# Layer 0's output projection weights: split once beside the gates' projections and reloaded in two parts, instead of split inside the attention

## The chip, the cores and the metric

One core of one Trainium2 chip. The metric is the device time of one execution in microseconds; lower is better.

## The reference

A two-layer diffusion backbone over 2048 image tokens and 256 context tokens, 1024 wide, all in float32. Cut to what matters here, for layer 0:

```python
hx = rms_norm(x, norm_pre[0]) * (1.0 + sc_x) + sh_x      # the same for the context, hc
px = hx @ w_in                                           # 1024 -> 8 branches of 512
out_a = diff_attention_post(o, subln, lam_init) * silu(ga)   # o: differential attention, 8 heads,
                                                             # 2048 queries on 2304 keys
out_b = short_conv(bb, cb, ub, conv_w) * silu(gb)
mx = concat([out_a, out_b])                              # 1024 wide
x = x + g_x * rms_norm(mx @ w_out[0], norm_post[0])      # the output projection; the same for the context
```

The change concerns `w_out[0]`, a 1024 x 1024 float32 matrix (4.19 MB).

## The kernel before

**Two parts of a number.** Most large products run as three matmuls on float32r, a rounded float32: a matrix is split into a high part (rounded to float32r) and a low part (what is left), and the product is high x high + high x low + low x high. So each weight matrix has to be split before use: a rounding copy and a subtraction.

**Stages of layer 0.** `in_proj0` projects the inputs block by block; its last stage is the gates, 8 weight blocks of 128 columns times 5 chunks of tokens, 40 gate blocks in all, each 24 matmuls. `run` does them one after the other: `split_w` for a new weight block, `project`, then a step of the modulation and those steps of the context's small attention (`ctx_attention`) whose turn it is. PSUM has four buffers for the blocks; ScalarE (ACT) takes each out with a Silu, and a store on SyncE's (SP's) queue writes it to DRAM, for `ga` and `gb`.

`attention0` follows. Its order is written out by hand: `ATT_ORDER` gives each operation of a period of four query tiles a due time in ns, the period is `ATT_PERIOD` = 36858, and 32 periods cover 8 heads. The due times are only an order: they fix in which sequence each engine gets its instructions (`pin`). The operations are QK (score matmuls, L1044), TR (reduce_scores on VectorE, L803), EX (exponentials on ACT, L1083), PS and PA (GpSimd scales and adds, L1103 and L1108), TP and EV (transposes, L1115, and their copies on ACT, L1122), AV (values, L1132). Scores have two PSUM buffers, so a QK waits for the TR two before it. F are slots in which TensorE gets matmuls of the short convolution (`conv_units`, L734) until they are used up. Extra steps are put in by `run_late(d, step)`: due d ns after the present due time.

When the convolution is used up, `after_conv` is called (6000 after it). It frees the convolution's SBUF, calls `load_wout(0, ...)`, and puts in, by due time from the call: the 16 splits; the gate rows (`gate_rows`, two small matmuls that spread a row over the partitions); and the first context block of the output projection (`out_first`: nine calls, of which the first loads the mixed activations, `load_mix`, and casts them on VectorE at L1353 and L1355, and eight do three matmuls each at L1275). 37 TR operations are still to come after the call, the last due 54544 after it.

`load_wout` issues sixteen loads of 256 KB on SP's queue and returns sixteen splits. Each is one GpSimd copy (L1250) and one VectorE subtraction (L1251) of 128x512, pinned into these engines' orders among the attention's operations:

```python
self.pin(nc.gpsimd.tensor_scalar(h, x, 1.0, 1.0, ALU.mult, ALU.mult))
self.pin(nc.vector.tensor_tensor(lw, x, h.bitcast(F32), ALU.subtract))
```

After the last QK the rest of the context's output projection (`out_ctx`) and then that of the image tokens (`out_proj`) fill TensorE beside the attention's last transposes and values. `load_wout` is also used for layer 1, inside its own attention.

Each engine executes its instructions in order, and so does SP's queue, which issues every transfer of the kernel.

Of the kernel before, what the change touches and what calls it, by code (L numbers as in the profile page):

```python
# [9 lines left out]
F32 = mybir.dt.float32  # L10
F32R = mybir.dt.float32r
AF = mybir.ActivationFunctionType
ALU = mybir.AluOpType
# [4 lines left out]
P = 128  # L18
# [3 lines left out]
D = 1024  # L22
# [14 lines left out]


ATT_PERIOD = 36858
Y0 = 7000  # L40

FILL = 430

WGAP, YGAP = 1900, 3900
ATT_ORDER = """
QK0000:0 QK0001:349 TR0000:1266 TR0001:3756 QK0002:3791 TR0002:4792 QK0010:5725 LS000:5986 TR0010:6919 F00:6946
QK0011:7446 QK0012:8231 TR0011:8375 F01:8580 LX00:9023 EX000:9323 TR0012:9411 QK0100:9734 F02:10083 TR0100:10447
# [65 lines left out]
class _Tags:  # L113


    def __init__(self, pool, tags, bufs=None):
        self.pool, self.tags, self.bufs = pool, tags, bufs or {}
# [37 lines left out]
class Backbone:  # L155
    def __init__(self, ctx, tc, a):
        self.ctx, self.tc, self.nc, self.a = ctx, tc, tc.nc, a
        self.wout = None
        self.na = {}
        self.cst = ctx.enter_context(tc.tile_pool(reuse_waits="tile", name="cst", bufs=1))  # L160
        self.dram = ctx.enter_context(tc.tile_pool(reuse_waits="tile", name="dram", bufs=1, space=DRAM))
        d = self.dram

        self.q_hl = d.tile([2, BW, T], F32, name="q")
        self.k_hl = d.tile([2, BW, T], F32, name="k")
        self.v = d.tile([T, BW], F32, name="v")
        self.ga = d.tile([BW, T], F32, name="ga")

        self.mixa = [[d.tile([BW, n], F32, name=f"mixa{l}{t0}") for t0, n in CHUNKS[:5 - l]] for l in range(2)]
        self.mixb = [d.tile([BW, T - L * l], F32, name=f"mixb{l}") for l in range(2)]  # L170
        self.x1 = d.tile([S, D], F32, name="x1")
        self.hx0 = [d.tile([P, 2, 8, 256], F32, name=f"hx0{i}") for i in range(9)]
        self.hx1 = [d.tile([P, 8, 256], F32, name=f"hx1{i}") for i in range(9)]
        self.gb = d.tile([BW, T], F32, name="gb")
        self.q1_hl = [d.tile([BW, S], F32, name=f"q1{i}") for i in range(2)]
        self.k1_hl = [d.tile([BW, T], F32, name=f"k1{i}") for i in range(2)]
        self.v1 = d.tile([T, BW], F32, name="v1")
        self.gn = d.tile([BW, S], F32, name="gn")
        self.gd = d.tile([BW, S], F32, name="gd")
        self.fd = [d.tile([P, 4, 512], F32, name=f"fd{b}") for b in range(4)]  # L180
        self.bt = d.tile([8 * 64 * 15 * 64], F32, name="bt")
# [27 lines left out]
    def load(self, dst, src):  # L209

        self.pin(self.nc.sync.dma_start(dst, src))
# [236 lines left out]
    def split_values(self, src, ring, full, c, pin=None):  # L448
# [6 lines left out]
        nc.scalar.activation(wh, full, AF.Copy)  # L455
        nc.vector.tensor_tensor(wl, full, wh.bitcast(F32), ALU.subtract)


    def in_proj0(self, sil):
        MODS = 31  # L460
        nc, a = self.nc, self.a
        W = a["w_in_even"][0]
        with ExitStack() as es:
            tp = self.pool(es, "tmp0", 2, "left")
# [36 lines left out]
            def keep_hx(ci, part):  # L501

                t0, n, x = hx[ci][0], hx[ci][1], hx[ci][2 + part]
                for c0 in range(0, n, 256):
                    nc.sync.dma_start(self.hx0[(t0 + c0) // 256][:, part], x[:, :, c0:c0 + 256].bitcast(F32))
# [6 lines left out]
                return tp.tile([P, n, 256], F32, tag="wm", name=name)  # L512

            mod = self.modulation(mods, tp, mp, pt, wtile)
            ctx_steps = []
            loaded = []
            n_ctx = [0]
# [2 lines left out]
            def run(units):  # L520

                ws = {}
                for (b, w_ap, emit), ci in units:
                    if b not in ws:
                        ws[b] = self.split_w(w_ap, pw)
                        loaded.append(b)
                        nb = len(loaded)
                        with self.tc.issue_after(ws[b][2].ins):
                            if nb > 3 and keep:
                                keep_hx(*keep.pop(0))  # L530
                            if nb == 4:
                                self.bias_fill(tp)
                            if 8 <= nb < 16:
                                self.bias_rows(nb - 8)
                    self.project(ws[b], hx[ci], pp, emit, self.pin)

                    n_run[0] += 1
                    if n_run[0] > 45 or n_run[0] * MODS % 45 < MODS:
                        next(mod, None)
                    while ctx_steps and ctx_steps[0][0] < n_ctx[0]:  # L540
                        ctx_steps.pop(0)[1]()
                    n_ctx[0] += 1
# [68 lines left out]
            with self.tc.issue_after(self.pinned[mybir.EngineType.SP]):  # L611
                values(0, (2, 3))
                for ci in order[2:]:
                    make_hx(ci)
                    values(ci, range(4))
                block = lambda c0, emit: (c0, W[:, c0:c0 + P], emit)
                run([(block(1024 + 3 * P, store_v(3)), ci) for ci in order])
# [7 lines left out]
            def store_qk(dst, cb):  # L625
# [18 lines left out]
                return emit  # L644

            run([(block(512 + cb * P, store_qk(self.k_hl, cb)), ci) for cb in range(4) for ci in order])
            run([(block(cb * P, store_qk(self.q_hl, cb)), ci) for cb in range(4) for ci in order])
            rs.close()
            cp = self.pool(es, "ax", 1, "left")
            ctx_steps += self.ctx_attention(cp, pt)  # L650
            n_ctx[0] = 0

            def store_gate(dst, cb):
# [11 lines left out]

            run([(g, ci) for ci in (4, 1, 2, 0, 3) for g in gates[5:]])
            assert next(mod, None) is None
            assert not ctx_steps and not keep


# [279 lines left out]
    def attention0(self, ws, xs, ys, ps_t, ps_o):  # L950


        nc, a, tc = self.nc, self.a, self.tc
# [6 lines left out]
        with ExitStack() as es:  # L960
# [4 lines left out]
            sp = self.pool(es, "as", 1, "left")  # L965
# [14 lines left out]
            kst, qst, vts, nxt = {}, {}, {}, {}  # L980
# [22 lines left out]
            now, late, last, norms = [0], [], [], {}  # L1003

            def run_late(d, *steps):
                late.extend((now[0] + d, s) for s in steps)
                late.sort(key=lambda x: x[0])
# [179 lines left out]

            def after_conv():
                cs.close()
                fp, steps = self.load_wout(0, ws, xs)  # L1190
                rows = self.gate_rows(0, 1, _Tags(fp, {"grow": "ws"}, {"grow": 2}), ps_t, ep, "sq")
                first = self.out_first(_Tags(ep, {"m0": "ob", "m1": "ob"}, {"m0": 6, "m1": 6}))
                for i, step in enumerate(steps):
                    run_late(6000 + WGAP * i, step)
                for i in range(3):
                    run_late(6000 + 16 * WGAP + 1000 * i, lambda: next(rows, None))
                for i in range(9):
                    run_late(Y0 + YGAP * i, lambda: next(first, None))

# [23 lines left out]
                step()  # L1223
        return last


    def load_wout(self, l, es, fs):

        nc = self.nc
        wp = self.pool(es, f"ow{l}", 1, "right")  # L1230
        self.wout = ([], [])
        fp = self.pool(fs, f"of{l}", 1, "right")

        full = []
        for kc in range(8):
            for hf in range(2):
                x = (fp.tile([P, 512], F32, tag="ws", name="ws", bufs=2) if kc == 7 else
                     full[-1] if hf else wp.tile([P, D], F32, tag=f"wl{kc + 1}", name="ws"))
                cs = slice(hf * 512, hf * 512 + 512)
                full.append(x)  # L1240
                nc.sync.dma_start(x if kc == 7 else x[:, cs], self.a["w_out"][l][kc * P:kc * P + P, cs])

        def split(kc, hf):
            if hf == 0:
                self.wout[0].append(wp.tile([P, D], F32R, tag=f"wh{kc}", name="wh"))
                self.wout[1].append(wp.tile([P, D], F32R, tag=f"wl{kc}", name="wl"))
            cs = slice(hf * 512, hf * 512 + 512)
            h, lw = [self.wout[i][kc][:, cs] for i in range(2)]
            x = full[2 * kc + hf] if kc == 7 else full[2 * kc + hf][:, cs]
            self.pin(nc.gpsimd.tensor_scalar(h, x, 1.0, 1.0, ALU.mult, ALU.mult))  # L1250
            self.pin(nc.vector.tensor_tensor(lw, x, h.bitcast(F32), ALU.subtract))  # L1251

        return fp, [lambda kc=kc, hf=hf: split(kc, hf) for kc in range(8) for hf in range(2)]
# [804 lines left out]
```

## Time and profile before

| | us |
|---|---|
| median of 3 runs | 3311.87 (3310.3 to 3313.59) |
| the profiled execution | 3307.55 |
| its span, first to last instruction | 3305.8 |
| TensorE busy in the span | 3159.8 (96%) |
| VectorE busy | 1923.2 (58%) |
| ScalarE busy | 1588.4 (48%) |
| GpSimd busy | 1452.5 (44%) |

Layer 0's gates run from about 384 to 600 us of the span, its attention from 600 to about 1925; the convolution's last matmul starts at 1804.7, and load_wout's first load is issued at 1809.71. All rows come from the profiled execution, whose own time stands beside its span. A busy share over the whole span is a mean over stages with different limits.

### The profile page before, as it was taken

Reading aid. Unit: us, or ns where it says so; the run is one execution under the profiler, and the core shown is the slowest. Engines: PE = TensorE matmul, PEld = TensorE weight load, DVE = VectorE, ACT = ScalarE, POOL = GpSimd, SP = SyncE. Lnnn points to the kernel's source line nnn. Section 1 sums busy time; section 2 is a strip of 40 time slices with the busy share of each in tenths; the row PEclk is TensorE's granted clock in tenths of the full one; section 3 lists DMA queues with packets and bytes.
Section 4 is the critical chain, followed back from the end, with each engine's and each line's share of the span. In section 5 each row is a group of like instructions: output and inputs, shape, how many; then the busy total and the mean of one; then the engine's idle time right before and its main releaser. Section 6 shows DMA issues by size and latency. Waiting matters only on the chain. (4 is left out here: it accounts for less than half of the span.)

```text
span 3305.8 us, 53754 instructions
## 1 busy us (share of the span) xinstructions
PE 3159.8 (96%) x20154; PEld 2614.0 (79%) x20154; DVE 1923.2 (58%) x4315; ACT 1588.4 (48%) x2541; POOL 1452.5 (44%) x1205
## 2 busy tenths in 40 slices
PE   7999999999999999989999799999999998899999
PEld 6988878778787878777777578898888887788887
DVE  4466663688888888888887745321121026566643
ACT  4311143577777878777777543421111124566410
POOL 3234200477887888777877743200121002343300
PEclk9999999999999999999999899999999999999999
DMA  7367643523333243323332144533232247953233
GB/s 259 125 209 238 213 147 117 177 100 112 132 118 118 90 157 98 123 91 114 117 98 76 52 157 157 178 106 126 70 112 95 90 147 223 226 146 107 69 136 121
DMA packets 305319, 442.08 MB, mean 134 GB/s; under 512 B 54838, under 2 KB 212002, under 8 KB 292259
## 3 DMA queue, kind: packets, MB, share of 16 engines
q1 hardware_dynamic: 305058, 438.64, 41.2%
q8 instruction: 160, 2.62, 0.3%
q14 instruction: 101, 0.82, 0.1%
HBM read 307.59 MB, written 131.43 MB: 133 GB/s over the span
## 5 line engine op out<-in xcount | busy, mean ns | idle before, releaser
L421 PE MATMUL mm<-hx,wh 128*128 128x512 f32 (+1 forms) x2784 | 828.9, 381 | 2.3 <-DVE lo L631 2.3
L803 DVE CUSTOM_DVE_ANT_0 s<-ps,zero 128x768 f32<-128x768 f32 x768 | 718.2, 952 | 167.2 <-PE ps L1044 161.9
L1108 POOL TENSOR_TENSOR s<-s 128x992 f32<-128x992 f32 x256 | 595.4, 2340 | 7.2
L421 PEld LDWEIGHTS mm<-hx,wh 128*128 128x128 f32 x2784 | 509.3, 188 | 108.9 <-DVE lo L631 2.7
L421 PE MATMUL mm<-hx,wl 128*128 128x512 f32 (+1 forms) x1392 | 529.6, 380 | 0.0
L1044 PE MATMUL ps<-kst,qst 128*128 128x512 f32 (+1 forms) x1536 | 430.4, 369 | 75.4 <-DVE mx L803 67.4
L1122 ACT ACTIVATE aT<-pt 128x512 f32<-128x512 f32 (+1 forms) x640 | 336.2, 549 | 151.7 <-PE pt L1115 150.5
L1103 POOL TENSOR_SCALAR s<-s,cf 128x992 f32<-128x992 f32 x256 | 300.7, 1185 | 244.3 <-DVE cf L1093 114.5
L734 PE MATMUL cmm<-cx,wh 128*128 128x256 f32 x1728 | 355.2, 292 | 6.1 <-ACT z L753 4.9
L1044 PEld LDWEIGHTS ps<-kst,qst 128*128 128x128 f32 x1536 | 237.3, 193 | 143.0 <-DVE mx L803 90.4
L1115 PE MATMUL pt<-sm,s 128*128 128x128 f32 x2304 | 340.0, 277 | 5.9 <-ACT aT L1122 5.4
L1083 ACT ACTIVATE s<-s,bias 128x2304 f32<-128x2304 f32 x128 | 284.4, 2221 | 52.6 <-DVE bias L1072 52.3
L421 PEld LDWEIGHTS mm<-hx,wl 128*128 128x128 f32 x1392 | 262.1, 188 | 53.7
L1115 PEld LDWEIGHTS pt<-sm,s 128*128 128x128 f32 x2304 | 270.5, 142 | 42.1 <-ACT aT L1122 13.0
L734 PEld LDWEIGHTS cmm<-cx,wh 128*128 128x128 f32 x1728 | 278.1, 193 | 17.5 <-ACT z L753 7.9
L1083 ACT ACTIVATE s<-s,low 128x2304 f32<-128x2304 f32 x128 | 283.5, 2215 | 2.1
L1132 PE MATMUL po<-aT,vt 128*64 128x256 f32 x2304 | 278.3, 386 | 0.8 <-DVE f L827 0.8
L734 PE MATMUL cmm<-cx,wl 128*128 128x256 f32 x864 | 249.1, 288 | 0.0
L1132 PEld LDWEIGHTS po<-aT,vt 128*64 128x64 f32 x2304 | 154.3, 137 | 94.5 <-issue 27.2
L1934 POOL TENSOR_SCALAR s<-s,rz 128x832 f32<-128x832 f32 (+1 forms) x128 | 123.0, 961 | 200.2 <-DVE rz L1933 148.7
L1275 PE MATMUL y<-wh,mh 128*128 128x512 f32 x544 | 182.5, 414 | 1.2 <-DVE mx L803 1.2
L1275 PE MATMUL y<-wh,mx 128*128 128x512 f32 x544 | 173.9, 398 | 0.0
(265 smaller groups left out, 4802.0 us busy)
## 6 DMA issues: line engine op xcount, KB each, us to landing
cx<-hx SPq DMA_DIRECT2D x72, 1024.0 KB
hx<-hx SPq DMA_DIRECT2D x18, 1024.0 KB
kst<-k SPq DMA_DIRECT2D x192, 96.0 KB
k<-k SPq DMA_DIRECT2D x32, 576.0 KB
xt<-in_x_dram SPq DMA_DIRECT2D x32, 512.0 KB
wm<-in_w_mod_dram SPq DMA_DIRECT2D x64, 256.0 KB
qst<-q SPq DMA_DIRECT2D x256, 64.0 KB
ws<-in_w_in_even_dram SPq DMA_DIRECT2D x27, 512.0 KB
```

The costliest lines, as they stand in the source:

```text
L421: mm = self.nc.tensor.matmul(ps[:, :n], p[:, kc], y, start=first, stop=last)
L734: yield nc.tensor.matmul(ps, w[p][:, kc, :], x[q][:, kc, :], start=i == 0, stop=i == 23)
L803: return self.nc.vector.tensor_tensor_reduce(dst, ps, self.zero.to_broadcast([P, n]), -QS, BIGGEST, ALU.add, ALU.min, mx)
L1044: pin(nc.tensor.matmul(ps[:, k0:k1], q[:, qc:qc + P], k[:, k0:k1], start=True, stop=True))
L1083: pin(nc.scalar.activation(it.s[m], it.s[m], AF.Exp, bias=bias, scale=-1.0, accum_out=it.Z if m else it.rz[:, 0:1]))
L1103: pin(nc.gpsimd.tensor_scalar(x, x, it.cf, 1.0, ALU.mult, ALU.mult))
L1108: pin(nc.gpsimd.tensor_tensor(it.s[0][:, cs], it.s[0][:, cs], it.s[1][:, cs], ALU.add))
L1115: pin(nc.tensor.transpose(pt[:, i * P:i * P + P], it.s[0][:, k0:k0 + P], self.ident))
L1122: pin(nc.scalar.activation(it.aT[g][:, 0:k, n * P:n * P + P], it.pt.pop(g)[:, 0:k * P].rearrange("p (k q) -> p k q", q=P), AF.Copy))
L1132: pin(nc.tensor.matmul(it.po[c:c + 64, 0:256], vts[it.h][:, kt, :], it.aT[g][:, i, :], start=kt < 2, stop=kt >= 16, tile_position=(0, c)))
L1275: self.pin(self.nc.tensor.matmul(ps[hf] if isinstance(ps, list) else ps[:, cs], x, w[kc][:, cs], start=kc == 0 and i == 0, stop=kc == 7 an ...
L1934: nc.gpsimd.tensor_scalar(s[:, :w], s[:, :w], rz, 1.0, ALU.mult, ALU.mult).ins]
```

## The change

- `in_proj0` gets a new generator, `split_later`, called once after each gate block. It walks over `w_out[0]` in 32 chunks of 128x256: the load of the next chunk is issued a step ahead into one of two halves of a staging tile; ACT rounds the present chunk into a high part (one buffer); VectorE subtracts in place for the low part; two stores write the parts to DRAM.
- `after_conv` calls `load_wout0` instead of `load_wout(0, ...)`: sixteen loads of 512 KB, high and low part of each of the eight row blocks, straight to their places. The sixteen splits inside the attention are gone. Layer 1 keeps `load_wout`.
- The due times of the first context block's steps change: `Y0` from 7000 to 8000, `YGAP` from 3900 to 4500. The gate rows are now due at a fixed place of the attention's period, which comes to 31628, 32628 and 33628 after the call instead of 36400, 37400 and 38400.

```diff
-Y0 = 7000
+Y0 = 8000
-WGAP, YGAP = 1900, 3900
+WGAP, YGAP = 2000, 4500
@@ Backbone.__init__
+        self.wo_hl = [[d.tile([P, D], F32, name=f"wo{kc}{p}") for p in range(2)] for kc in range(8)]
@@
+    def split_later(self, sp, tp):
+        nc = self.nc
+        todo = [(self.a["w_out"][0][kc * P:kc * P + P, c0:c0 + 256], [x[:, c0:c0 + 256] for x in self.wo_hl[kc]])
+                for kc in range(8) for c0 in range(0, D, 256)]
+        def load(i):
+            x = place[:, i % 2 * 256:i % 2 * 256 + 256]
+            nc.sync.dma_start(x, todo[i][0])
+            return x
+        place = tp.tile([P, 512], F32, tag="eh", name="sl", bufs=1)
+        nxt = load(0)
+        yield
+        for i, (_, dst) in enumerate(todo):
+            full, hi = nxt, sp.tile([P, 256], F32R, tag="sl1", name="sl", bufs=1)
+            if i + 1 < len(todo):
+                nxt = load(i + 1)
+            lo = full.bitcast(F32R)
+            nc.scalar.activation(hi, full, AF.Copy)
+            nc.vector.tensor_tensor(lo, full, hi.bitcast(F32), ALU.subtract)
+            for x, y in zip(dst, (hi, lo)):
+                nc.sync.dma_start(x, y.bitcast(F32))
+            yield
@@ in_proj0
+            parts = iter(())
                     self.project(ws[b], hx[ci], pp, emit, self.pin)
+                    next(parts, None)
             ctx_steps += self.ctx_attention(cp, pt)
+            parts = self.split_later(self.pool(es, "sl", 1, "left"), tp)
             assert next(mod, None) is None
+            for _ in parts:
+                pass
@@ after_conv
-                fp, steps = self.load_wout(0, ws, xs)
+                fp = self.load_wout0(ws, xs)
-                for i, step in enumerate(steps):
-                    run_late(6000 + WGAP * i, step)
+                d = WGAP + (13000 - now[0] - WGAP) % ATT_PERIOD
                 for i in range(3):
-                    run_late(6000 + 16 * WGAP + 1000 * i, lambda: next(rows, None))
+                    run_late(d + 1000 * i, lambda: next(rows, None))
@@
+    def load_wout0(self, es, fs):
+        wp = self.pool(es, "ow0", 1, "right")
+        self.wout = ([], [])
+        for kc in range(8):
+            for i, t in enumerate(("wh", "wl")):
+                x = wp.tile([P, D], F32R, tag=f"{t}{kc}", name=t)
+                self.nc.sync.dma_start(x.bitcast(F32), self.wo_hl[kc][i])
+                self.wout[i].append(x)
+        return self.pool(fs, "of0", 1, "right")
```

## Rows read from the trace of the kernel before

**Rows 1.** The page, part 1: busy us (share of the span) and instructions.

```profile
PE 3159.8 (96%) x20154; PEld 2614.0 (79%) x20154; DVE 1923.2 (58%) x4315; ACT 1588.4 (48%) x2541; POOL 1452.5 (44%) x1205
```

**Rows 2.** Busy us by stretch: PE, PEld, DVE, ACT, POOL; granted clock, DMA share, GB/s.

```profile
1804.70:1816.10 11.40, 10.31 (x71) 7.56 (x69) 10.11 (x26) 10.79 (x15) 10.68 (x8) 1.00 0.51 173
1811.00:1891.20 80.20, 57.83 (x329) 40.27 (x327) 65.63 (x130) 48.08 (x72) 61.33 (x44) 0.89 0.20 66
1877.70:1891.20 13.50, 10.63 (x72) 7.47 (x70) 11.91 (x32) 11.12 (x19) 10.45 (x7) 1.00 0.02 5
1891.20:1932.00 40.80, 39.98 (x233) 29.39 (x234) 15.66 (x27) 17.14 (x32) 23.07 (x19) 1.00 0.36 125
```

**Rows 3.** Waits from 1804 to 1891: us in total, times, longest.

```profile
PE ps L1044 <- DVE mx L803: 19.1, 17, 4.2
...
DVE wl L1251 <- POOL wh L1250: 5.7, 5, 1.4
```

**Rows 4.** Groups by line, VectorE, 1811 to 1891.2: busy us, mean ns, idle before.

```profile
L803 DVE CUSTOM_DVE_ANT_0 s<-ps,zero 128x768 f32<-128x768 f32 x37 | 34.5, 951 | 5.8 <-PE ps L1044 5.7
L1251 DVE TENSOR_TENSOR wl<-ws,wh 128x512 fp32r<-128x512 f32 x16 | 21.7, 1355 | 5.7 <-POOL wh L1250 5.7
```

**Rows 5.** Groups by line, GpSimd, 1811 to 1891.2.

```profile
L1108 POOL TENSOR_TENSOR s<-s 128x992 f32<-128x992 f32 x13 | 29.8, 2303 | 0.2
...
L1250 POOL TENSOR_SCALAR wh<-ws 128x512 fp32r<-128x512 f32 x16 | 13.3, 837 | 0.0
```

**Rows 6.** VectorE in order of time: start us, us.

```profile
1819.44 0.69 DVE L1251 TENSOR_TENSOR wl<-ws,wh 128x512 fp32r<-128x512 f32 x1
...
1827.33 1.17 DVE L1353 CAST mh<-mx 128x512 fp32r<-128x512 f32 x1
...
1853.17 2.76 DVE L1251 TENSOR_TENSOR wl<-ws,wh 128x512 fp32r<-128x512 f32 x1 [1.24 <-POOL wh L1250]
```

**Rows 7.** GpSimd in order of time.

```profile
1853.10 2.27 POOL L1108 TENSOR_TENSOR s<-s 128x992 f32<-128x992 f32 x1
```

**Rows 8.** 5 us stretches, the same columns.

```profile
1810.00:1815.00 5.00, 4.79 (x37) 3.30 (x36) 3.75 (x10) 4.56 (x8) 4.92 (x4) 1.00 0.87 299
1815.00:1820.00 5.00, 4.47 (x33) 2.66 (x31) 3.60 (x10) 3.23 (x6) 3.97 (x4) 1.00 0.92 305
1820.00:1825.00 5.00, 2.63 (x13) 1.73 (x13) 4.18 (x6) 3.20 (x5) 5.00 (x5) 1.00 1.06 374
...
1830.00:1835.00 5.00, 3.97 (x17) 3.43 (x18) 3.92 (x9) 1.33 (x3) 2.29 (x3) 0.59 0.02 3
...
1850.00:1855.00 5.00, 2.27 (x15) 1.60 (x13) 3.73 (x6) 3.85 (x6) 5.00 (x4) 0.95 0.01 2
```

**Rows 9.** SyncE's queue in order of time.

```profile
1809.71 10.47 SPq L1241 DMA_DIRECT2D ws<-in_w_out_dram  x16
1820.53 0.38 SPq L1351 DMA_DIRECT2D mx<-mixb  x1
```

**Rows 10.** Groups by line, whole span: 128x256 copy and subtraction.

```profile
L695 ACT ACTIVATE wh<-ws 128x256 fp32r<-128x256 f32 (+1 forms) x37 | 13.3, 425 | 2.3 <-PE cmm L734 1.5 <-DMA ws<-in_w_in_even_dram 0.8
...
L631 DVE TENSOR_TENSOR lo<-mm,hi 128x256 fp32r<-128x256 f32 x8 | 3.4, 423 | 22.7 <-ACT hi L630 9.9 <-DMA k<-t 7.2 <-DMA q<-t 5.6
```

**Rows 11.** Stretches of layer 0's gates.

```profile
400.00:420.00 20.00, 15.88 (x73) 12.64 (x73) 12.05 (x39) 7.96 (x16) 0.00 (x0) 0.94 0.81 247
...
440.00:460.00 20.00, 20.00 (x97) 16.18 (x96) 12.31 (x41) 7.83 (x16) 0.00 (x0) 1.00 0.45 138
...
580.00:600.00 20.00, 20.00 (x89) 16.16 (x88) 1.65 (x2) 3.54 (x5) 0.74 (x1) 1.00 0.82 234
```

**Rows 12.** ScalarE in order of time, and what ended its idle time.

```profile
406.79 0.60 ACT L656 ACTIVATE g<-mm 128x512 f32<-128x512 f32 x1 [6.14 <-DMA ga<-g]
```

**Rows 13.** TensorE in order of time.

```profile
414.33 0.41 PE L916 MATMUL cpt<-sm,cs 128*128 128x128 f32 x2 [1.43 <-DVE czi L904]
417.42 0.62 PE L916 MATMUL cpt<-sm,cs 128*128 128x128 f32 x2 [2.68 <-DVE cs L907]
```

## The prediction

> **What bounds the kernel now.** I read the page first. TensorE (PE) is busy 96% of the span [rows 1], so work taken from another engine pays only where PE waits for that engine. I therefore looked along the span for the stretch where PE is not full and the edited lines run. The table by stretches gives it [rows 2]: from 1811.0 to 1891.2 us PE is busy 57.83 of 80.2 us, and the granted clock averages 0.89. Right after, from 1891.2 to 1932.0, PE is busy 39.98 of 40.8. So the 80.2 us are a trough between two full stretches, and what shortens the trough brings everything behind it forward. This is the end of layer 0's attention: the short convolution that filled PE is used up at 1804.7, and the output projection has not begun except for its first row block.
>
> Inside the trough PE waits for VectorE (DVE): score matmuls (L1044) wait for DVE's reduction L803, which frees their PSUM bank, 19.1 us in 17 waits, and DVE itself waits 5.7 us for GpSimd (POOL) at L1251 [rows 3]. By line DVE has 37 reductions, 34.5 us, and 16 weight subtractions L1251, 21.7 us [rows 4]; POOL spends 13.3 us on the 16 rounding copies L1250 besides its attention work [rows 5]. These 32 instructions are load_wout's split, and they are pinned into the two engines' orders among the attention's.
>
> The subtraction has two prices: 0.69 us alone, and 2.76 us at 1853.17 [rows 6], which is 0.69 plus almost the whole 2.27 us addition that POOL started at 1853.10 [rows 7]. DMA was at a share of 0.01 then [rows 8], so DMA traffic did not stretch it.
>
> **The change part by part.**
>
> *The split leaves the trough.* DVE loses 21.7 us of work and 5.7 us of waits there, 27.4 us; POOL loses 13.3. What is left over the 80.2 us, from the stretch's row [rows 2]: DVE 65.63-21.7 = 43.9, POOL 61.33-13.3 = 48.0, ACT 48.1, and PE 57.83 x 0.89 = 51.5 at the full clock. The clock fell to 0.59 in 1830-1835 [rows 8], a mix of the two levels of 1.2 and 2.4 GHz, while PE had waits in the trough, and those waits go. PE is then the longest, and the trough cannot be shorter than 51.5 us: the gain is at most 28.7. How full will PE be? From 1804.7 to 1816.1, with the convolution gone and the split not yet on DVE, it was busy 10.31 of 11.4 us, 90%; at the end, 1877.7 to 1891.2, with no split but the pipeline just refilling, 10.63 of 13.5, 79% [rows 2]. At 90% the trough is 57 us and the gain 23; at 79% it is 65.4 and the gain 14.8. I take 90%, because the first stretch is the same steady mix without the disputed work, and the second follows a stall. Term: -23, bounds -28.7 and -14.8.
>
> *Twice the bytes.* The sixteen 256 KB loads become sixteen of 512 KB, 8.39 MB where 4.19 were. Before, issuing starts at 1809.71 [rows 9], and DMA moves 299, 305 and 374 GB/s in the three 5 us stretches, mean 326 [rows 8]. At that rate the last weights land about 25.7 us after 1809.7, near 1835.4. PE needs them later: the first row block's eight steps are due 12.5 to 44 us after the loads' call (Y0 + YGAP i; all of the attention's remaining reductions fall within 54.5 us of it), about 1824 to 1857 at a 57 us trough, and its first pair of 1.05 MB lands after 3.2 us. So weights cost PE nothing; if that cover of 11 us at the first step were gone, the step would hold PE for what is missing.
>
> What is late next is the convolution's half of that row block: its load is issued behind the weights in the same queue (at 1820.53, after the sixteen) [rows 9], and so lands near 1836 where it was usable at 1827.33, when DVE's cast took it without waiting [rows 6]. DVE works in order: if the cast stands in its queue ahead of that landing, the reductions behind it wait, and the score matmuls behind those. The order after the change is not in this trace. Bounds: 0 if the cast stands behind the landing; about 13 if it keeps the place it had, eight reductions after the loads' start, which a faster trough reaches near 1823. In this kernel the cast came about 2 us after the traffic ended [rows 6, 8], so I place it near the landing: +2.
>
> The Trainium skill (DMA: Bandwidth & Descriptors, Specifications) gives 358 GB/s as HBM's limit for one core. By it 8.65 MB would take 24.2 us, an estimate, and land near 1834; the traced mean lands it near 1836, so the two differ by 2 us in this one term. A second page (SBUF — State Buffer, Who interferes with whom) says that engines and DMA cannot contend in SBUF, while DVE and POOL can lock each other out of a shared port pair. The trace agrees, 2.76 us at a DMA share of 0.01; were it otherwise, some 11 us of doubled traffic would also slow the reductions.
>
> *Retiming.* The first block's steps spread over 44 instead of 38.2 us, and the gate rows (two outer products and their casts) move from 36.4 to about 31.6 us behind the call. It is the same work inside the trough, already in the 51.5: 0.
>
> *The split beside the gates.* 32 steps, one after each of the first gate blocks: a 128 KB load one step ahead, an ACT copy of 128x256 (0.43 us by the convolution's weights), a DVE subtraction (0.42 by the same shape and operation) [rows 10], two 128 KB stores. That is 13.6 us of ACT and 13.4 of DVE spread over some 180 us in which PE is full: 20.00 of 20 in 440-460, with DVE 12.31, ACT 7.83 and DMA share 0.45, and so on to 580-600 [rows 11]. PE has four PSUM banks of slack, so the arithmetic is hidden. The queue is less free. SP issues 96 more transfers, in order with the gates' stores, the modulation's loads and the context attention's small loads, and 12.6 MB are added. At 400-420 DMA is already at 0.81 and PE busy only 15.88 of 20 [rows 11]: ACT stood 6.14 us until a gate store had landed [rows 12], and the context attention's transposes then held PE 1.43 and 2.68 us, 4.1 together [rows 13]. In the split a chunk's high part has one buffer, so each ACT copy waits for the previous store. With a round trip like that one, 6.14 + 0.43 = 6.6 us per step against about 5.4 for a gate block (24 matmuls; 89 run in the 20 us of 580-600 [rows 11]), ACT loses some 1.2 us a step while the queue is crowded. For the 3.7 steps of that 20 us stretch it is 4.4 us of ACT, and at the row's ratio (4.1 of PE for 6.14 of ACT) 3 us of PE. Afterwards, at 0.45, I expect none. Bounds 0 and, if every step loses 1.2 us, 32 x 1.2 x 4.1/6.14 = 26. I take +3.
>
> *Sum.* -23 + 2 + 3 = -18. The profiled execution took 3307.55 us against a span of 3305.8; the median of the runs shown is 3311.87, 4.3 above it. I subtract from both: 3289.6 for an execution like the profiled one, 3294 for the median.
>
> **The rivals.**
> 1. *The doubled loads hold DVE.* The cast stands early and DVE waits up to 13 us in the trough, so the gain is 23 - 13 - 3 = 7, some 3305. For it: one queue, in order, twice the bytes. Against: the cast did not wait before.
> 2. *SP's queue in the gate stage.* The one that ends slower. Each split step holds ACT behind its own store, and the context attention passes it to PE at 4.1 us for each 6.14 of ACT. From six such holds on (24.6 us) it outweighs the gain of 23; if all 32 steps lose 1.2 us and the trough gains only 14.8, the result is 26 + 2 - 14.8 = +13, near 3325. For it: the 400-420 stretch. Against: PE is full in each of the eight 20 us stretches from 440 to 600, and the first and the last leave ACT more than half idle [rows 11].
> 3. *The trough does not shorten.* POOL and ACT (48 us each) are in lockstep with PE, and removing the split turns DVE's work into waits for them; the gain is under 5 and the kernel lands near 3308 to 3312. For it: the chain of an attention tile passes all four engines. Against: the 90% stretch.
>
> **How the numbers follow.** Likeliest (trough down 15 to 28, small costs) 0.66; rival 1 0.14, of which 0.11 is still past the 0.2% that a measurement of this kernel can tell from no change (6.6 us); rival 2 0.12, 0.07 slower and 0.05 within 0.2%; rival 3 0.08, 0.03 of it faster. Faster is 0.66 + 0.11 + 0.03 = 0.80, same 0.03 + 0.05 + 0.05 = 0.13, slower 0.07. The low end takes the floor of PE with little cost, -27: 3285; the high end takes rivals 1 and half of 3, 3309. The likeliest case alone is 3285 to 3302.
>
> **What would show it.** Right: no L1250 or L1251 work in layer 0's trough, the last reduction L803 55 to 62 us after the loads start instead of 81, PE's waits on L803 there under 10 us, granted clock above 0.95, and everything behind shifted by the same amount. The weights' traffic lasts some 26 us. In the gate stage, PE's idle time grows by 0 to 6 us over the 4.1. Wrong: DVE idle before the cast until DMA lands (rival 1); ACT or SP waiting on the split's own stores, and attention starting 10 us or more later (rival 2); PE as idle as before but waiting for ACT's copies L1122 or POOL's sums L1108 (rival 3).

## The result and the profile after

The changed kernel took 3329.43 us (median of 6 runs, 3325.76 to 3334.42) against 3312.73 for the kernel before on the same chip (6 runs, 3304.98 to 3317.66): a ratio of 1.0054 [1.0041, 1.0068], slower by 0.54%. The forecast was 3294, the range 3285 to 3309: wrong in sign. The profiled execution took 3325.76 us, its span 3324.0, which is 18.2 above the 3305.8 of before.

Read in the stretches in which the prediction argued, the 18.2 us fall apart like this (us, before to after):

| stretch | before | after | difference |
|---|---|---|---|
| span's start to the first gate Silu | 384.0 | 390.6 | +6.6 |
| first to last gate Silu (the gate stage) | 219.8 | 260.9 | +41.1 |
| to the first QK | 0.6 | 0.7 | +0.1 |
| first QK to the convolution's last matmul | 1200.2 | 1192.7 | -7.5 |
| from there to the last reduction (the trough) | 85.6 | 65.0 | -20.6 |
| to the end | 1415.6 | 1414.1 | -1.5 |

**The trough.** The kernel after, stretches (us; busy us of PE, PEld, DVE, ACT, POOL; granted clock, DMA share, GB/s): first the end of the convolution, then from 1.3 us after the weights' first load, then the time of the loads and 5 us out of its middle:

```profile
1845.10:1856.60 11.50, 10.30 (x71) 7.56 (x70) 10.06 (x26) 10.88 (x15) 10.78 (x8) 1.00 0.58 203
1851.30:1910.90 59.60, 51.80 (x328) 37.18 (x326) 48.60 (x113) 47.67 (x72) 47.73 (x28) 0.97 0.42 159
1850.00:1874.50 24.50, 23.05 (x161) 16.52 (x161) 18.75 (x48) 21.32 (x32) 22.37 (x13) 1.00 0.98 375
1860.00:1865.00 5.00, 4.07 (x25) 3.02 (x24) 4.46 (x11) 4.75 (x10) 4.79 (x3) 1.00 1.02 415
```

Its waits from 1851.3 to 1910.9 (us in total, times, longest):

```profile
PE ps L1077 <- DVE mx L836: 5.2, 6, 2.5
```

The same operations in order of time, on SyncE's queue and on VectorE (two views):

```profile
1850.01 0.32 SPq L1267 DMA_DIRECT2D wh<-wo  x1
...
1863.43 0.32 SPq L1267 DMA_DIRECT2D wl<-wo  x1
1864.71 0.37 SPq L1395 DMA_DIRECT2D mx<-mixb  x1
```

```profile
1877.38 0.76 DVE L1397 CAST mh<-mx 128x512 fp32r<-128x512 f32 x1
```

Against [rows 2] DVE's load fell from 65.63 us in 80.2 to 48.60 in 59.6, PE is busy 87% instead of 72%, the clock is 0.97 instead of 0.89, and PE's wait for the reductions fell from 19.1 us [rows 3] to 5.2. While the doubled loads (8.39 MB) ran, all traffic of the core came to 375 GB/s over 24.5 us, and the cast behind them took its input without a wait.

**The gate stage.** Stretches of the whole stage, the kernel before and then the kernel after:

```profile
384.00:603.80 219.80, 215.55 (x1090) 176.28 (x1089) 100.17 (x317) 78.53 (x156) 8.30 (x10) 0.99 0.52 159
```

```profile
390.60:651.50 260.90, 228.47 (x1091) 184.85 (x1089) 113.11 (x349) 89.67 (x187) 7.41 (x10) 0.93 0.60 182
```

PE's idle time grew from 4.3 to 32.4 us, by 28.2. The other 12.9 of the 41.1 are in PE's busy time: the same matmuls took longer at a lower granted clock. By 20 us, the kernel after, answering to [rows 11]:

```profile
400.00:420.00 20.00, 12.78 (x65) 10.92 (x64) 9.88 (x31) 3.82 (x9) 0.00 (x0) 0.76 0.72 214
...
480.00:500.00 20.00, 13.88 (x73) 11.05 (x72) 11.44 (x35) 9.83 (x21) 1.12 (x1) 0.83 0.70 207
...
560.00:580.00 20.00, 13.21 (x64) 11.69 (x64) 9.72 (x32) 6.04 (x15) 1.01 (x1) 0.73 0.52 162
```

Of the stage's rows these three are the ones in which PE stood longest, and none has a lower clock (a mix of 1.2 and 2.4 GHz). What it stood for, from the waits of 380 to 660, first all engines, then SyncE's queue:

```profile
ACT sl L480 <- DMA wo<-sl: 63.9, 19, 8.8
DVE sl L481 <- ACT sl L480: 55.7, 21, 4.8
...
ACT wh L406 <- DMA ws<-in_w_in_even_dram: 17.2, 4, 6.5
...
PE cps L927 <- DMA cqk<-k: 12.0, 3, 7.2
...
PE cpt L949 <- DVE cs L940: 10.1, 5, 5.8
...
PE mm L423 <- ACT wh L406: 4.0, 3, 3.1
```

```profile
SPq L690 <- ACT g L687: 14.5, 9, 5.2
SPq L468 <- DMA wo<-sl: 13.7, 15, 3.2
SPq L483 <- ACT sl L480: 13.3, 9, 3.3
```

The waits of rival 2 are there: ACT stands 63.9 us behind the split's own stores. But the largest of PE's own waits, 12.0 us, is for something else, the context attention's small loads `cqk`. Next come 10.1 us of the context attention's transposes waiting for DVE, the kind of hold that the prediction priced (4.1 before [rows 13]), and 4.0 us in which the gates' own matmuls wait for the split of their weights, whose loads `ws` stand in SyncE's queue too. `cqk` by tile, the kernel before and then the kernel after (count; duration in ns min/median/max; first and last start; "who waited for it"):

```profile
L798 SPq DMA_DIRECT2D cqk<-k x64: 302/420/977, 385.6 to 524.7; - x64
...
who waited for it (us, times):
  DVE cs L803: 7.2, 2
```

```profile
L831 SPq DMA_DIRECT2D cqk<-k x64: 302/420/1539, 393.2 to 562.7; - x64
...
who waited for it (us, times):
  PE cps L927: 13.5, 4
  PEld cps L927: 9.2, 2
```

No matmul waited for them before; now PE and its weight loads do, 13.5 and 9.2 us, and the last one is issued 38.0 us later. (The two waits can overlap: in run 8 they add to 27.1 us where PE idles 24.3. So their sum is no share of PE's idle time.) Why it is late stands in SyncE's queue in order of time; below it TensorE at the same place:

```profile
407.50 0.46 SPq L287 DMA_DIRECT2D wm<-in_w_mod_dram  x1
408.00 0.97 SPq L831 DMA_DIRECT2D cqk<-q  x2
409.80 0.35 SPq L468 DMA_DIRECT2D sl<-in_w_out_dram  x1
410.25 0.85 SPq L483 DMA_DIRECT2D wo<-sl  x2
411.20 0.43 SPq L690 DMA_DIRECT2D ga<-g  x1
411.68 1.86 SPq L831 DMA_DIRECT2D cqk<-k  x4
```

```profile
407.77 0.36 PE L927 MATMUL cps<-cqk 128*128 128x256 f32 x1
415.35 0.98 PE L927 MATMUL cps<-cqk 128*128 128x256 f32 x3 [7.22 <-DMA cqk<-k]
```

PE stands from 408.1. The four loads that it needs are issued only at 411.68, after a split load that first waited 0.8 us, two split stores and a gate store; then they take their own 1.86 us of issuing and the way to SBUF. Compare [rows 13]: the holds at about this time were 1.43 and 2.68 us, and of another kind, transposes that waited for DVE.

### The profile page after: what moved, and what is told of

It reads as the page before. It is cut to its first block, busy times and chain, and to the rows that moved or that the text cites. A ratio compares the mean times of both kernels' runs of the same rounds, so it can differ in the third digit from the quotient of the medians.

```text
span 3324.0 us, 53982 instructions
## 1 busy us (share of the span) xinstructions
PE 3161.7 (95%) x20154; PEld 2614.7 (79%) x20154; DVE 1917.5 (58%) x4331; ACT 1598.6 (48%) x2573; POOL 1438.4 (43%) x1189
## 3 DMA queue, kind: packets, MB, share of 16 engines
q1 hardware_dynamic: 318882, 455.42, 42.5%
## 4 chain that ended last, share of the span: by engine, by line
PE 68%; DVE 11%; DMA 8%; issue 7%; ACT 2%; SPq 2%; POOL 1%; DVEq 0%; ACTq 0%; POOLq 0%
PE mm L423 18%; PE cmm L767 8%; PE po L1165 7%; PE ps L1077 7%; PE y L1319 6%; PE pt L1148 6%; PE mm L435 5%; DVE s L836 4%; PE po L2017 3%; PE ps L1966 3%; PE pt L2000 2%; DMA wo<-sl 1%; PE pc L1807 1%; DVE me L308 1%; DMA be<-bt 1%
## 5 line engine op out<-in xcount | busy, mean ns | idle before, releaser
L767 PEld LDWEIGHTS cmm<-cx,wh 128*128 128x128 f32 x1728 | 276.0, 192 | 17.3 <-ACT z L786 7.9
L767 PE MATMUL cmm<-cx,wl 128*128 128x256 f32 x864 | 248.1, 287 | 0.0
```

The lines of the kernel that those rows point to most:

```text
L767: yield nc.tensor.matmul(ps, w[p][:, kc, :], x[q][:, kc, :], start=i == 0, stop=i == 23)
```

## The experiments

The theories: **H** (rival 2 as forecast): ACT and DVE stand at the split's few buffers and hold what is behind them. **Q**: the context attention's loads come late, for which there are two reasons, **Q1**, SyncE issues in order and has no time left, and **Q2**, the split's 12.6 MB of loads and stores crowd the DMA engines. All gate stages and idle times below are read as above; the table stands behind the runs.

**1. The trough alone.** The split beside the gates is left out.

```diff
-            parts = self.split_later(self.pool(es, "sl", 1, "left"), tp)
...
-                self.nc.sync.dma_start(x.bitcast(F32), self.wo_hl[kc][i])
+                self.nc.sync.dma_start(x.bitcast(F32).rearrange("p (k c) -> p k c", c=256), self.hx0[kc][:, i, 0:4])
```

> The split beside the gates is left out, and the sixteen 512 KB loads read other data of the same size (parts of the activations' two halves), so the output projection of layer 0 multiplies by wrong weights: it has the right number of matmuls, bytes and steps. It shows what the trough gains by itself. Both theories (H: in the gate stage ScalarE and VectorE stand at the split's own few buffers and hold what is queued behind them; Q: SyncE's queue and the extra traffic delay the context attention's loads whatever the engines do) put the whole loss into the gate stage, so both expect attention to start within 3 us of before (604), the last reduction of layer 0 some 20 to 30 us earlier than before, and a time of 3283 to 3293. A third theory, that the changed loads or the new due times also cost something later, expects above 3300.

Measured: 3289.4 us, 0.9932 [0.9916, 0.9947] of before, -22.3. Attention started at 610.9 and not within 3 us of 604, but the gate stage is that of before (220.5 against 219.8): the first gate Silu was already 5.7 us later. The trough, from the convolution's last matmul to the last reduction, and below it that of run 2, which keeps the old trough:

```profile
1811.60:1875.50 63.90, 56.12 (x366) 40.49 (x364) 53.75 (x126) 52.29 (x80) 52.44 (x33) 1.00 0.43 155
```

```profile
1850.00:1935.60 85.60, 63.58 (x366) 44.92 (x364) 70.93 (x144) 52.88 (x80) 66.09 (x49) 0.90 0.20 67
```

**2. The gate split alone.** The parts are written but not read; the loads, the splits and the due times in the trough are those of before.

```diff
-                fp = self.load_wout0(ws, xs)
+                fp, steps = self.load_wout(0, ws, xs)
...
+                for i, step in enumerate(steps):
+                    run_late(6000 + WGAP * i, step)
```

> The split beside the gates is kept, its results are written to DRAM and not used, and the weights are loaded and split inside the attention as before, with the due times of before. H and Q: the cost of the gate stage alone, some 40 to 50 us, so 3353 to 3363, with attention starting near 650. If instead the two halves of the change work on each other (the third theory), the sum of this run's loss and the gain of the run without the gate split differs from the changed kernel's +17 by more than 6 us.

Measured: 3354.43 us, 1.0133 [1.0114, 1.0152], +42.7. The two halves add to +20.4 where the whole is +16.7: they act apart, within 4 us.

**3. More buffers.** Four places for high parts and three for chunks, loads two steps ahead.

```diff
...
-            full, hi = nxt, sp.tile([P, 256], F32R, tag="sl1", name="sl", bufs=1)
-            if i + 1 < len(todo):
-                nxt = load(i + 1)
+            full, hi = nxt[i], his[i % 4]
+            if i + 2 < len(todo):
+                nxt.append(load(i + 2))
```

> The changed kernel with four buffers for the high part instead of one and three places for the staged chunks instead of two, so loads go two steps ahead. The same 96 transfers and the same engines. H: ScalarE no longer waits for the store of the chunk before (63.9 us in 19 waits in the changed kernel); attention starts by 620 and the time is 3285 to 3303. Q: the transfers are the same, the context's loads come as late as now; attention starts at 640 or later and the time stays at 3318 to 3332.

Measured: 3327.96 us, 1.0046 [1.0031, 1.006]; the stage 253.4. ACT no longer stands at its own stores, but at the loads, and PE still at `cqk`. So ACT's wait was moved and not removed; the test of H is run 4. The wait here:

```profile
ACT sh L481 <- DMA sl<-in_w_out_dram: 51.1, 19, 9.2
```

**4. The split's arithmetic on GpSimd**, its transfers still on SyncE. ACT and DVE have no part in it.

```diff
-            nc.scalar.activation(hi, full, AF.Copy)
-            nc.vector.tensor_tensor(lo, full, hi.bitcast(F32), ALU.subtract)
+            nc.gpsimd.tensor_scalar(hi, full, 1.0, 1.0, ALU.mult, ALU.mult)
+            nc.gpsimd.tensor_tensor(lo, full, hi.bitcast(F32), ALU.subtract)
```

> The changed kernel with both operations of the split beside the gates on GpSimd, which is nearly idle there (2.6 of 20 us at most), with the same single buffer, two halves and 96 transfers. ScalarE and VectorE have nothing of the split. H: attention starts by 615 and the time is 3283 to 3298. Q: SyncE still waits for the same stores in its order; attention starts at 635 or later and the time is 3315 to 3332.

Measured: 3323.88 us, 1.0044 [1.0026, 1.0061]; the stage 256.2. With ACT and DVE free of the split, 36 of the 41 us remain: H is not the main cause. The stage of this run, and below it that of run 6:

```profile
387.80:644.00 256.20, 228.32 (x1092) 185.45 (x1090) 108.65 (x317) 78.45 (x155) 47.38 (x74) 0.93 0.62 186
```

```profile
388.80:618.40 229.60, 216.01 (x1086) 176.01 (x1084) 107.17 (x317) 78.45 (x155) 99.52 (x168) 0.98 0.68 207
```

**5 and 6. The transfers on GpSimd's queue**: in run 5 the arithmetic stays on ACT and DVE, in run 6 it is on GpSimd too (the diff of 4 added).

```diff
-            nc.sync.dma_start(x, todo[i][0])
+            nc.gpsimd.dma_start(x, todo[i][0])
...
-                nc.sync.dma_start(x, y.bitcast(F32))
+                nc.gpsimd.dma_start(x, y.bitcast(F32))
```

> The changed kernel with the 96 transfers of the gate-side split issued from GpSimd's queue instead of SyncE's; ScalarE and VectorE split as in the changed kernel, same buffers, same bytes. H (the engines stand at the split's few buffers) is weakened by the last two runs, Q is now parted. Q1: SyncE, which issues every transfer in order, is the bound of the gate stage (219 transfers of 0.46 us each in 184 us before, and most of the rest spent waiting in order); what counts is the number of its transfers and their waits. It expects attention to start by 618 and 3285 to 3302. Q2: the 12.6 MB of added traffic on the shared DMA engines delays the context attention's loads, whoever issues it: attention starts at 635 or later, 3315 to 3335.

> As the run before, and both operations of the split on GpSimd too, so that neither SyncE nor ScalarE nor VectorE has anything of it. Q1: attention starts by 612 and the time is 3284 to 3296; if it is faster than the run before by more than 4 us, the engines' waits at the split's buffers (H) were a part of the loss. Q2: as before, 635 or later, 3315 to 3335.

Measured: run 5 3315.26 us, 1.001 [0.9997, 1.0024], the stage 241.4; run 6 3300.66 us, 0.9969 [0.9957, 0.998], the stage 229.6. Run 5 falls between the theories: attention starts at 629.6 (Q1 by 618, Q2 from 635), and the time is past Q1's and at the edge of Q2's. Run 6 starts attention at 619.0 and is a little past Q1's bounds, far from Q2's. Same bytes, same number of transfers, same engines for run 4 and run 6: the other queue takes 26.6 us off the stage. With ACT and DVE in it (after against run 5) it takes 19.5. In run 5 nothing on PE waits for `cqk` any more, but PE is idle 17.7 us for other reasons: there the part of ACT and DVE comes to 11.8 us (run 5 against run 6), where it came to 4.7 behind the slow queue (after against run 4). One thing else differs between run 4 and run 6, the packets. Part 3 of the two pages, run 4 and then run 6 (packets, MB, share of the DMA engines):

```profile
q1 hardware_dynamic: 318882, 455.42, 43.2%
```

```profile
q1 hardware_dynamic: 305058, 442.83, 42.3%
q0 software_dynamic: 4608, 12.59, 1.2%
```

SyncE's queue moved the split's 12.6 MB in 13824 packets, GpSimd's in 4608. Run 8 looks at what packets can cost.

**7. Half the transfers**, each twice as large (16 chunks of 512 columns, one at every second gate block, in two staging tiles), on SyncE, ACT and DVE.

```diff
-                for kc in range(8) for c0 in range(0, D, 256)]
+                for kc in range(8) for c0 in range(0, D, 512)]
...
-            full, hi = nxt, sp.tile([P, 256], F32R, tag="sl1", name="sl", bufs=1)
+            full = nxt
+            yield
```

> The changed kernel with 16 chunks of 512 columns instead of 32 of 256, a chunk after every second gate block: 48 transfers instead of 96 on SyncE's queue, the same 12.6 MB. Q1: about half of the loss, attention starts between 618 and 634, 3298 to 3314. Q2: the same traffic, attention starts at 638 or later, 3318 to 3334.

Measured: 3306.87 us, 0.9987 [0.9973, 1.0]; the stage 238.6, 22.3 us under that of the changed kernel with the same bytes, though with half the packets too.

**8. Small transfers**: the 96 transfers carry 16 columns each, a sixteenth of the bytes.

```diff
-            nc.sync.dma_start(x, todo[i][0])
+            nc.sync.dma_start(x[:, 0:16], todo[i][0][:, 0:16])
...
-                nc.sync.dma_start(x, y.bitcast(F32))
+                nc.sync.dma_start(x[:, 0:16], y[:, 0:16].bitcast(F32))
```

> The same 96 transfers at the same places on SyncE's queue, but each moves 16 of its 256 columns, 0.8 MB in all instead of 12.6; the staged chunks are zeros elsewhere, and the reloads read other data as in the run of the trough alone, so layer 0's output projection has wrong weights. Q1: the loss stays, attention starts at 630 or later and the time is 3312 to 3332. Q2: the traffic is gone, attention starts by 615, 3285 to 3300.

Measured: 3319.44 us, 1.0024 [1.0011, 1.0037]; the stage 248.1. The packets are as many as in the changed kernel (318882 on SyncE's queue), but the DMA share is 0.51, that of before (0.52). With nearly no bytes, 28.3 of the 41.1 us remain. So it is the transfers' number and place in the queue, Q1, more than what they carry. The stage, and `cqk` by tile:

```profile
387.20:635.30 248.10, 223.79 (x1079) 182.46 (x1078) 112.57 (x349) 89.86 (x187) 7.65 (x10) 0.94 0.51 144
```

```profile
who waited for it (us, times):
  PE cps L928: 14.8, 4
  PEld cps L928: 12.3, 3
```

**9 to 11. A later start of the split.** All three have transfers and arithmetic on GpSimd. Run 9 calls the generator only from the eighth gate block on, run 10 does so with the wide chunks of run 7, and run 11 is run 9 with the first load put behind TensorE's last pinned matmul (the last three lines of the diff).

```diff
-                    next(parts, None)
+                    if n_ctx[0] >= 7:
+                        next(parts, None)
...
-        nxt = load(0)
+        with self.tc.issue_after(self.pinned[mybir.EngineType.PE]):
+            nxt = load(0)
```

> As the run with everything of the gate-side split on GpSimd, but its steps begin seven gate blocks later, behind the crowded stretch in which the input activations are stored. In that run what is left of the loss is about 9 us of the gate stage, most of TensorE's idle time between 400 and 440. Q2a (the added traffic costs only where the DMA engines are already full): the gate stage is within 4 us of the kernel before and the time is 3288 to 3296. Q2b (it costs wherever it runs): the loss stays, 3298 to 3304.

> The same, with 16 chunks of 512 columns instead of 32 of 256: half the transfers and half the GpSimd instructions, the same bytes. Both theories expect it within 3 us of the other run of this call; if it is more than 4 us faster, the number of transfers costs on GpSimd's queue as well.

> The version with everything of the split on GpSimd, begun seven gate blocks later, with its first load now held until TensorE's last matmul of the seventh gate block, so that its transfers cannot start with the gate stage as they did in the run before (388.2 us). Q2a (the 16.8 MB of extra traffic cost only in the crowded first 50 us, 388 to 440, where the context attention's loads are late): the split starts after 425 us and the gate stage falls from 229.6 to within 3 us of the 220.5 that it takes without a split, so the kernel lands 6 to 9 us under the version with everything on GpSimd, near 3291 to 3294 on its scale of 3300.7. Q2b (the extra traffic costs the same wherever it stands): the gate stage stays at 228 to 232 us and the time within 3 us of 3300.7. If the tail of the split now runs past the last gate block, the attention's start waits for nothing of it, and the weights' reload is 1200 us later, so a late end costs nothing in either theory.

Measured: run 9 3306.72 us, 0.9986 [0.9973, 0.9999]; run 10 3310.7 us, 1.0001 [0.9991, 1.0011]; run 11 3300.44 us, 0.9985 [0.9973, 0.9998]. The edit did not do what it was for: the split's loads still begin with the gate stage. Run 11, by line:

```profile
L468 POOL DMA_DIRECT2D sl<-in_w_out_dram x32: 541/541/794, 389.0 to 563.3; - x32
```

In run 6 they run from 387.1 to 563.2, in run 9 from 384.5 to 558.0. So where the traffic costs its share was not told apart. What the three do give is a repetition: runs 6, 9 and 11 are nearly one kernel, with gate stages of 229.6, 230.0 and 228.9 us and ratios from 0.9969 to 0.9986. Run 10 missed its forecast, which was within 3 us of run 9: its median is 4.0 us longer, its stage 8.2 (238.2), and PE waits for `cqk` again. So on GpSimd's queue half the transfers of twice the size gained nothing; why was not followed up. (The 16.8 MB of the last expectation take in the 4.2 MB more that the reload reads; beside the gates it is 12.6.)

| kernel | gate stage | PE idle in it | last `cqk` load issued | waits for `cqk`, PE's plus PEld's (they overlap) | trough |
|---|---|---|---|---|---|
| before | 219.8 | 4.3 | 524.7 | none | 85.6 |
| after | 260.9 | 32.4 | 562.7 | 22.7 | 65.0 |
| 1 trough alone | 220.5 | 5.5 | 531.2 | none | 63.9 |
| 2 gate split alone | 260.1 | 32.9 | 562.6 | 23.4 | 85.6 |
| 3 more buffers | 253.4 | 29.7 | 556.2 | 22.2 | 65.0 |
| 4 arithmetic on GpSimd | 256.2 | 27.9 | 558.7 | 17.3 | 64.9 |
| 5 transfers on GpSimd | 241.4 | 17.7 | 547.5 | none | 64.9 |
| 6 both on GpSimd | 229.6 | 13.6 | 538.3 | none | 65.0 |
| 7 half the transfers | 238.6 | 16.0 | 546.7 | 12.0 | 63.9 |
| 8 small transfers | 248.1 | 24.3 | 550.3 | 27.1 | 64.9 |
| 9 later start | 230.0 | 13.7 | 536.5 | none | 65.0 |
| 10 later start, half the transfers | 238.2 | 17.9 | 549.6 | 15.3 | 65.0 |
| 11 first load held | 228.9 | 13.5 | 540.5 | none | 65.0 |

(Times of issue are from each span's start; the stages start between 384.0 and 390.6. Each row is one execution.)

## Why the prediction was wrong

**The trough was right.** Forecast -23 for the split's removal and +2 for what the doubled loads delay; measured -20.6 in the trough, and -22.3 for the whole of run 1. (The +2 was not measured by itself.) PE's share, taken as 90%, came to 87%; the last reduction started 60 us after the loads (forecast 55 to 62); the clock is 0.97 (above 0.95); the waits for the reductions are 5.2 us (under 10). Rival 3 is out. So is rival 1: the loads ended near 1874.5, 24.5 us after their start (forecast some 26), and the cast at 1877.38 found its input there. The 358 GB/s that the Trainium skill (DMA: Bandwidth & Descriptors, Specifications) gives as one core's limit at HBM did not bind here: the rows show 375 for all traffic over these 24.5 us and 415 in 5 us of their middle, and the measurement decides.

**The step that failed is "the split beside the gates", +3 with bounds 0 and 26; it cost +41.1.** Two things in it were wrong, and one was left out.

1. *What was priced.* The step counted SyncE's 96 transfers and named what is in line with them, and then priced only ACT's hold behind its own store: "For the 3.7 steps of that 20 us stretch ... Afterwards, at 0.45, I expect none." The 0.45 is the share of the DMA engines' time. It tells nothing of the queue that issues, which is a resource of its own. Added up over SyncE's queue, from the first gate Silu to the last `cqk` load: before, 140.7 us for 200 transfers, of which 90.8 issuing, 44.6 waiting and 5.3 neither; after, 172.1 us for 281, of which 128.0 issuing, 36.4 waiting and 7.7 neither. The last load is 31.4 us later in the stage, and that is 37.2 more of issuing, 8.2 less of waiting and 2.4 of the rest. Of the 36.4 the split's own waits (L468 and L483) are 16.0, so the waits of before shrank from 44.6 to 20.4: the queue had some slack and used it, and it was too little. By the same count run 8, with 281 transfers, issued for 127.0 us, and run 6, with 200, for 92.5. The hold that was priced was too small as well, 63.9 us of ACT in 19 waits against 1.2 us a step, but it is not what cost most.
2. *What passes it on.* The ratio 4.1 of PE for 6.14 of ACT came from one place in the crowded stretch and stood for ACT's hold. Rival 2 rested on the same hold. Its heading was the right one and so was its sign; its mechanism is the smaller part. In steps that can be taken one behind the other: ACT and DVE out of the split -4.7 us (after to run 4, which the times do not tell from nothing: 1.0054 [1.0041, 1.0068] and 1.0044 [1.0026, 1.0061]), the transfers off SyncE -26.6 (run 4 to run 6), the rest of the split -9.1 (run 6 to run 1). Of the last, the bytes are one candidate: run 6 has 12.6 MB more than run 1 and at 400 to 420 us a DMA share of 0.99 (run 1: 0.88). That it is the bytes was not shown. What PE waits for most in run 6 are the context attention's transposes behind DVE, 10.2 us (run 1: 5.5), the place that the prediction had looked at. The order matters by some us: with the transfers moved first, ACT and DVE cost 11.8.
3. *The clock.* The step counted only waits. Of the 41.1 us, 12.9 are the same matmuls at a mean clock of 0.93 instead of 0.99, on top of 28.2 of added idle time, which alone is past the upper bound of 26. The ratio of the two is not fixed: in run 6, 9.3 us of added idle time came with 0.5 us (216.01 busy at a clock of 0.98).

The evidence against, "PE is full in each of the eight 20 us stretches", was read as slack. It shows that PE did not wait, not how early the loads came. The row to look for was the queue's own: how much of the stretch SyncE spends issuing, and how much it stands.

The Trainium skill (Trainium Kernel Development and Optimization, Key Constraints) says that transfers issued from SP, ACT and POOL share the same 16 DMA engines, so that several issuing engines save only the sequencer's issue time. Runs 4 and 6 put a number to that "only": 26.6 us, less whatever the fewer packets gave. That the two queues share their DMA engines no run here shows.

**A version that beats both.** Run 6 keeps the change and takes its transfers and its arithmetic to GpSimd, which is busy 7.41 us in the stage otherwise: 0.9969 [0.9957, 0.998] of before; its near copies gave 0.9986 and 0.9985. Run 1 shows the limit, 0.9932, if the split cost nothing.

**What stays open.** The stage between the first QK and the convolution's end took from 1191 to 1203 us in the thirteen kernels, 7.5 less after than before, and the first gate Silu came 384.0 us after the start before and between 386.2 and 390.6 in all others, though run 1 changes nothing ahead of it. Neither was followed up. The profiled execution of before is 5.2 us quicker than the median of that kernel (3307.55 against 3312.73), so a difference of a few us between two single executions may be no more than scatter. How the last 9.1 us divide is open as well, and so is what the fewer packets of GpSimd's queue saved.

## What to carry to other kernels

A queue that issues transfers is an engine: before adding transfers to it, add up its issue times and its waits over the stretch, as for any other engine, and ask which small load behind them has a reader that cannot wait. A low DMA share says nothing about that. Where such a queue has too little slack, fewer and larger transfers (run 7) or another engine's queue (run 6) give time back; the two together did not add up (run 10). A wait that this spares TensorE can be worth more than its own length: here 28.2 us of idle time came with 12.9 us of slower matmuls.

## What was not expected of the hardware

- Issuing a 128 KB transfer held SyncE 0.37 to 0.38 us in the median (L468 and L483 after); with a sixteenth of the bytes (run 8) it was 0.39 and 0.38. GpSimd took 0.54 and 0.59 us for the same two (run 6).
- 28.2 us of added idle time on PE, in pieces of up to 7.2 us, came with a mean granted clock of 0.93 instead of 0.99 over the stage; 9.3 us in run 6 came with 0.98.
- All traffic of the core came to 375 GB/s (DMA share 0.98) over the 24.5 us of sixteen 512 KB loads, against a mean of 326 in the prediction's three stretches, with sixteen of 256 KB.
- The same 12.6 MB went in 13824 packets from SyncE's queue and in 4608 from GpSimd's.
